# Seven running totals of a Strassen-style MLP product: which of them are quarters of the result, in which order the others are folded into them, and on which engine

## The chip, the cores and the metric

One core of a Trainium2 chip. The metric is the device time in microseconds of one execution, the median of the runs shown. Engines are called by the names of the profile: PE is TensorE, DVE is VectorE, ACT is ScalarE, POOL is GpSimd, SP is SyncE, whose queue starts all the transfers here.

## What is computed

One decoder layer on 1024 tokens of 1024 features in float32: an attention branch and an RWKV-7 branch, merged, then an MLP, then a gated per-layer embedding. The end of it, where the change lies:

```python
f = rmsnorm(h, ffn_pre_norm[i])
f = jnp.square(jax.nn.relu(f @ w_ff_in[i])) @ w_ff_out[i]     # 1024 -> 4096 -> 1024
h = h + rmsnorm(f, ffn_post_norm[i])
e = (p[i] @ w_ple[i]) * jax.nn.sigmoid(h @ w_ple_gate[i])
h = h + rmsnorm(e, ple_post_norm[i])
```

## The kernel before

**Precision.** Each float32 matmul is three matmuls of rounded operands (`mm3`, L250): high x high, high x low, low x high, into one PSUM bank of 128 x 512. An operand is split by ScalarE (a copy that rounds, the high part) and by VectorE or GpSimd (a subtraction, the low part).

**The MLP's second product.** The 4096 hidden features are taken in 16 chunks of 256 (`NP` = 16, p = 0 to 15). For a chunk the 1024 x 256 activations and the 256 x 1024 weights are cut into two by two quarters, and for the first 15 chunks Strassen's seven products replace the eight: each product of the order `MUL` (L1292) takes sums of quarters (`LEFT`, `RIGHT`; `prep` and `split2` make and split them ahead of time on GpSimd, ScalarE and VectorE) and gives four tiles of 128 x 512. `product` (L1371) multiplies them in five rotating PSUM banks and adds each to a running total of its own, `tot[1]` to `tot[7]`, on VectorE: the line `tot<-tot,bk` of the profile, called an eviction here. The last chunk, p = 15, is multiplied plainly, 16 tiles of six matmuls (`ff2_last`, L1435, three banks), added into the quarters of the result. `acc(i, c)` (L1308) says which total holds the quarter of token tile i and column half c.

**The folds.** With totals M1 to M7, the quarters are M1 + M4 - M5 + M7, M3 + M5, M2 + M4 and M1 - M2 + M3 + M6. In `product` of chunk 14 (the branch at L1385), after the products 4, 1 and 7, the totals are folded into the four that `acc` names: eight steps on four tiles of 128 x 512 each, 32 operations, the rows `tot<-tot,tot`; even tiles on GpSimd, odd ones on VectorE.

**Around them.** `ff1` (L1392) interleaves, for each 128 hidden features j, the first product (w_ff_in, banks `z`, two token halves of 24 matmuls) with the products of the chunk before: twelve matmuls of `z`, one product, and so on. So the last stretch of TensorE is: product 2, z, product 4, z, product 1, z, product 7, z, then the 16 tiles of `ff2_last`. `last_split` (L1325) splits the operands of chunk 15 beside them (`lhl` in four pieces on VectorE; `lwl` in two of 128 x 1024, the first on VectorE, the second on GpSimd). `last_weights` (L1450) loads w_ple_gate in eight pieces of 128 rows into two raw buffers (`wr`) and splits each: the left column half on GpSimd, the right half on VectorE (`wsplit`, L1177; rows `wpg<-wr,wpg`). `finish(i)` (L1476) normalises token tile i, adds the residual, and transposes it; `gate_mm(i)` (L1491) multiplies it by the gate weights, the left half first (24 matmuls), then the right half; `e_mm(i)` makes the output.

**Order.** TensorE's order is written out by the kernel's own planner (`Order`, with assumed durations). The context is entered with a manual schedule for TensorE alone:

```python
ctx.enter_context(tc.manual_schedule(engines={mybir.EngineType.PE}))   # L217
```

The queues of the other engines and of SP are ordered by the compiler. Each engine executes its queue in order. A buffer's `tag` says which storage it shares with earlier tiles: `last_split`'s second `lwl` takes the storage (`MP`) of the right operand of product 1, the gate weights' right halves take that of the second token half of f, which the last matmuls `z` read.

Of the kernel before, what the change touches and what calls it, by code (L numbers as in the profile page):

```python
# [13 lines left out]
OP = mybir.AluOpType  # L14
# [192 lines left out]
def layer(ctx: ExitStack, tc: tile.TileContext, x, pT, wz, wup, w_out, wff1, w_ff2, w_ple, w_pleg,  # L207
# [5 lines left out]
    V = Engine(nc.vector, sch, 0.18, 0.00104)  # L213
    S = Engine(nc.scalar, sch, 0.16, 0.00092)
    G = Engine(nc.gpsimd, sch, 0.15, 0.0022)
# [34 lines left out]
    def mm3(ps, pairs):  # L250
        n = len(pairs)
        for i, (ah, al, bh, bl) in enumerate(pairs):
            PE.matmul(ps, ah, bh, start=i == 0, stop=False)  # L253
            yield MM
            PE.matmul(ps, ah, bl, start=False, stop=False)  # L255
            yield MM
            PE.matmul(ps, al, bh, start=False, stop=i == n - 1)  # L257
            yield MM
# [142 lines left out]
    def rtile(shape, name, tag, dt=F32):  # L401
        n = 1
        for d in shape[1:]:
            n *= d
        assert n <= TAGN[tag], (shape, tag)
        return rt.tile(shape, dt, name=name, tag=tag, bufs=BUFS.get(tag, 1))
# [52 lines left out]
    for h in range(2):  # L459
        for n, t in ((0, xw), (1, xg)):  # L460
            ps = zl[h][n]
            c = slice(P_MUX + n, P_MUX + n + 1)
# [636 lines left out]
    def mtile(p, h, shape, name, dt):  # L1099
        return mgpool().tile(shape, dt, name=name, tag=f"mt{p}{h}")  # L1100
# [5 lines left out]
    def bank(tags=("s1", "s2", "s3")):  # L1106
        zi[0] += 1
        return psum.tile([128, 512], F32, name="bk", tag=tags[zi[0] % len(tags)])
# [156 lines left out]
    def mixed(i, ps):  # L1265
# [16 lines left out]
        for c in range(2):  # L1282
# [8 lines left out]
    NP = FF // 256  # L1291
# [2 lines left out]
            7: (2, 3, OP.subtract)}  # L1294
    RIGHT = {1: (0, 3, OP.add), 2: (0,), 3: (1, 3, OP.subtract), 4: (2, 0, OP.subtract), 5: (3,),
             6: (0, 1, OP.add), 7: (2, 3, OP.add)}
    tot = {}
    raw_h, raw_w, duo = {}, {}, {}
    last = {}

    def totals():
        for p, (x, y) in enumerate(((4, 3), (2, 6))):
            t = mtile("hl"[p], 1, [128, 2, 4, 512], f"tot{p}", F32)
            tot[x], tot[y] = t[:, 0], t[:, 1]
        for x, tag in ((1, "BT"), (5, "AR0"), (7, "AR1")):
            tot[x] = rtile([128, 4, 512], "tot", tag)

    def acc(i, c):  # L1308
        return tot[((4, 3), (2, 6))[i // 4][c]][:, i % 4]

    def ff1_half(ps, hi, lo, h):
        return mm3(ps, [(hi[:, k * 128:(k + 1) * 128], lo[:, k * 128:(k + 1) * 128],
# [2 lines left out]
    def ff1_evac(ps, j, h):  # L1315
        p, x = j // 2, 2 * (j % 2) + h
        if p not in raw_h:
            raw_h[p] = rtile([128, 4, 512], "hr", ("BK", "UV")[p % 2])
        f1 = rtile([128, 512], "f1", "gst")
        S.activation(f1, ps, AF.Relu)  # L1320
        S.activation(raw_h[p][:, x], f1, AF.Square)
        if x == 3 and p == NP - 1:
            last_split(1, (1,), ())

    def last_split(k, hs, ws):  # L1325

        if k not in last:
            if k == 0:
                last["h"] = rtile([128, 4, 512], "lh", "BK", F32R)
                last["w"] = rtile([128, 2, 1024], "lw", "BK2", F32R)  # L1330
            last[k] = (rtile([128, 2, 512], "lhl", ("Ep", "En")[k], F32R),
                       rtile([128, 1024], "lwl", ("kk", "MP")[k], F32R))
        for h in hs:
            x = 2 * k + h
            S.activation(last["h"][:, x], raw_h[NP - 1][:, x], AF.Copy)
            V.tensor_tensor(last[k][0][:, h], raw_h[NP - 1][:, x], last["h"][:, x], OP.subtract)
        for _ in ws:
            S.activation(last["w"][:, k], raw_w[NP - 1][k], AF.Copy)
            (G if k else V).tensor_tensor(last[k][1], raw_w[NP - 1][k], last["w"][:, k], OP.subtract)

    def load_w2(p):
        if p % 2:
# [18 lines left out]
    def prep(n):  # L1361
        p, i = n // 7, MUL[n % 7]
        if p >= NP - 1:
            return
        hq = [raw_h[p][:, x] for x in range(4)]
        wq = [raw_w[p][x // 2][:, halves[x % 2]] for x in range(4)]
        pick = lambda q, spec: [q[x] for x in spec[:2]] + list(spec[2:])
        duo[n] = (split2(pick(hq, LEFT[i]), ("Ep", "En", "a")[n % 3], ("ex", "py")[n % 2], V),
                  split2(pick(wq, RIGHT[i]), ("kk", "MP", "px")[n % 3], "pg", G))

    def product(n):  # L1371
        p, i = n // 7, MUL[n % 7]
        prep(n + 2)
        a, b = duo.pop(n)
        if not tot:
            totals()
        for t in range(4):
            ts = slice(t * 128, t * 128 + 128)
            ps = bank(("s1", "s2", "s3", "m0", "m1"))
            yield from mm3(ps, [(a[:, 0, ts], a[:, 1, ts], b[:, 0], b[:, 1])])  # L1380
            if p == 0:
                V.tensor_copy(tot[i][:, t], ps)
            else:
                V.tensor_tensor(tot[i][:, t], tot[i][:, t], ps, OP.add)
        if p == NP - 2:  # L1385
            for x, y, op in {4: ((6, 3, OP.add), (6, 2, OP.subtract), (3, 5, OP.add), (2, 4, OP.add),
                                 (4, 5, OP.subtract)),
                             1: ((6, 1, OP.add), (4, 1, OP.add)), 7: ((4, 7, OP.add),)}.get(i, ()):
                for t in range(4):
                    (V if t % 2 else G).tensor_tensor(tot[x][:, t], tot[x][:, t], tot[y][:, t], op)  # L1390

    def ff1(j):  # L1392
        def body(hi, lo):
# [41 lines left out]
    def ff2_last(i, c):  # L1435
        def body():
            h, ts = tok(i)
            ps = bank()
            yield from mm3(ps, [(last["h"][:, 2 * k + h, ts], last[k][0][:, h, ts], last["w"][:, k, halves[c]],
                                 last[k][1][:, halves[c]]) for k in range(2)])  # L1440
            V.tensor_tensor(acc(i, c), acc(i, c), ps, OP.add)
            if i + c == 0:
                last_weights()
            if c == 1:
                sch.spawn(finish(i), 1)
        sch.add(body)
# [29 lines left out]
    def finish(i):  # L1476
        yield from wait(lambda: i == 0 or i - 1 in hT and (i < 2 or ("G", i - 2) in done))
        a = [acc(i, 0), acc(i, 1)]
        r = ss2(a, [rtile([128, 512], "j", "gst") for c in range(2)])
        for c in range(2):  # L1480
            hl = rtile([128, 512], "hl", ("ex", "py")[c])
            SY.dma_start(hl, h_scr[i][:, halves[c]])
            V.scalar_tensor_tensor(a[c], a[c], r, P["g3"][:, halves[c]], op0=OP.mult, op1=OP.mult)
            V.tensor_tensor(a[c], a[c], hl, OP.add)
        yield sch.until(sch.dep + 0.3)
        hi = wpool.tile([128, KT, 128], F32R, name="wh")
        lo = wpool.tile([128, KT, 128], F32R, name="wl")
        yield from put_T(a, hi, lo, 0)
        hT[i] = (hi, lo, sch.dep + 0.1)
# [18 lines left out]
    def e_mm(i):  # L1508
        def body():
            ts = slice(i * 128, i * 128 + 128)  # L1510
            sg, eg = P["sg"][i % 4], P["eg"][i % 3]
            cols = halves if i < 7 else (halves[0], slice(512, 768), slice(768, 1024))
            sc = small.tile([128, 4], F32, name="sc")
            for n, c in enumerate(cols):
                ps = bank()[:, 0:c.stop - c.start]
                yield from mm3(ps, [(P["p"][0][k][:, ts], P["p"][1][k][:, ts], P["w"][0][k][:, c],
                                     P["w"][1][k][:, c]) for k in range(2)])
                V.tensor_tensor(sg[:, c], sg[:, c], ps, OP.mult)
                S.activation(ps, sg[:, c], AF.Square, accum_out=sc[:, n:n + 1])
                (V if n else G).tensor_tensor(eg[:, c], sg[:, c], P["g4"][:, c], OP.mult)  # L1520
                if n:
                    V.tensor_tensor(sc[:, n:n + 1], sc[:, n - 1:n], sc[:, n:n + 1], OP.add)
            r = rstd_of(sc[:, n:n + 1], "rs")
            for c in cols:
                V.scalar_tensor_tensor(sg[:, c], eg[:, c], r,
                                       acc(i, c.start // 512)[:, c.start % 512:(c.stop - 1) % 512 + 1], op0=OP.mult, op1=OP.add)
                SY.dma_start(out[i * 128:(i + 1) * 128, c], sg[:, c])
        sch.add(body, None, lambda: ("G", i) in done)
# [125 lines left out]
```

## Time and profile before

| | |
|---|---|
| median of 3 runs | 1854.36 us (1851.88 to 1858.59) |
| the profiled execution | 1856.02 us, its span 1854.2 us |
| TensorE busy | 1771.5 us (96%), 9392 matmuls |
| VectorE busy | 1072.1 us (58%) |
| ScalarE busy | 750.0 us (40%) |
| GpSimd busy | 717.0 us (39%) |
| mean granted TensorE clock | 0.978 of full speed |

Busy shares are means over the span. Times in the rows are microseconds from the start of the span; an arrow in brackets at the end of a row gives how long the engine was idle ahead of it and what released it.

### The profile page before, as it was taken

The numbers are of one execution on the slowest core, as the hardware profiler recorded it, in microseconds if no ns is written. First come the engines' busy times: TensorE is split into PE (matmuls) and PEld (weight loads), VectorE is DVE, ScalarE is ACT, GpSimd is POOL, SyncE is SP. The second block draws the span as 40 slices with busy tenths as digits, with TensorE's granted clock in tenths as the row PEclk, the third lists the DMA queues.
The fourth block names the chain that finished last, engine by engine and source line by source line (L and its number), as shares of the span: only waits on it lengthen the run. The fifth ranks groups of instructions, "written<-read, shape, count | busy, mean of one in ns | idle before, by whom it ended". The sixth has DMA issues, their size and how long they took to land.

```text
span 1854.2 us, 24541 instructions
## 1 busy us (share of the span) xinstructions
PE 1771.5 (96%) x9392; PEld 1425.7 (77%) x9392; DVE 1072.1 (58%) x2005; ACT 750.0 (40%) x1358; POOL 717.0 (39%) x475
## 2 busy tenths in 40 slices
PE   9998998899899999999999999999999999996998
PEld 8777777686677777777778788888888888885787
DVE  6375794967744333334753655555555555579654
ACT  5923334323344444344433533333333333333454
POOL 1422222121113233332230166666666666685301
PEclk9998999999999999999999999999999999998999
DMA  4621221121223222233542311111111111111321
GB/s 158 235 72 46 66 83 36 63 75 54 92 89 96 80 58 57 69 100 105 190 159 80 114 57 46 57 46 57 69 46 46 46 57 46 57 40 62 114 75 51
DMA packets 54999, 146.03 MB, mean 79 GB/s; under 512 B 6625, under 2 KB 13281, under 8 KB 54882
## 3 DMA queue, kind: packets, MB, share of 16 engines
q1 hardware_dynamic: 54882, 144.46, 23.4%
q8 instruction: 74, 1.21, 0.3%
q14 instruction: 43, 0.35, 0.1%
HBM read 110.49 MB, written 27.26 MB: 74 GB/s over the span
## 4 chain that ended last, share of the span: by engine, by line
PE 72%; DVE 8%; ACT 2%; issue 1%; POOL 1%; DMA 0%; DVEq 0%; SPq 0%; ACTq 0%; POOLq 0%
PE z L255 15%; PE z L257 15%; PE z L253 15%; PE bk L253 6%; PE bk L255 6%; PE bk L257 6%; DVE tot L100 1%; DVE xy L100 1%; PE po L236 1%; PE sc L236 1%; PE y L236 1%; DVE pt L100 1%; PE pt L244 1%; PE q L236 1%; PE tp L244 1%
## 5 line engine op out<-in xcount | busy, mean ns | idle before, releaser
L100 DVE TENSOR_TENSOR tot<-tot,bk 128x512 f32<-128x512 f32 x408 | 276.8, 686 | 225.9 <-PE bk L257 225.9
L100 POOL TENSOR_TENSOR wl<-wr,wh 128x1024 fp32r<-128x1024 f32 (+1 forms) x88 | 209.6, 2382 | 505.1 <-ACT wh L100 500.4
L253 PE MATMUL z<-uh,wh 128*128 128x512 f32 (+1 forms) x800 | 318.5, 398 | 2.6 <-ACT v L100 1.9
L255 PE MATMUL z<-ul,wh 128*128 128x512 f32 (+1 forms) x800 | 319.2, 399 | 0.3 <-DVE ul L100 0.3
L257 PE MATMUL z<-uh,wl 128*128 128x512 f32 (+1 forms) x800 | 319.2, 399 | 0.2 <-POOL wl L100 0.2
L253 PE MATMUL z<-f,wh 128*128 128x512 f32 x512 | 200.3, 391 | 1.9 <-ACT f L100 1.9
L255 PE MATMUL z<-f,wh 128*128 128x512 f32 x512 | 200.3, 391 | 0.2 <-DVE f L100 0.2
L257 PE MATMUL z<-f,wl 128*128 128x512 f32 x512 | 199.9, 390 | 0.0
L253 PEld LDWEIGHTS z<-uh,wh 128*128 128x128 f32 x800 | 152.8, 191 | 31.5 <-issue 3.4
L257 PEld LDWEIGHTS z<-uh,wl 128*128 128x128 f32 x800 | 152.9, 191 | 31.2 <-issue 5.4
L100 ACT ACTIVATE duo<-sum 128x512 fp32r<-128x512 f32 x150 | 89.5, 624 | 214.8 <-PE bk L257 122.6
L255 PEld LDWEIGHTS z<-ul,wh 128*128 128x128 f32 x800 | 152.8, 191 | 30.4 <-issue 5.3
L253 PE MATMUL bk<-duo 128*128 128x512 f32 x420 | 164.3, 391 | 7.3 <-DVE tot L100 7.3
L100 ACT ACTIVATE wh<-wr 128x1024 fp32r<-128x1024 f32 (+1 forms) x88 | 91.6, 1041 | 186.8 <-PE z L255 168.9
L255 PE MATMUL bk<-duo 128*128 128x512 f32 x420 | 164.1, 391 | 0.0
L257 PE MATMUL bk<-duo 128*128 128x512 f32 x420 | 164.1, 391 | 0.0
L100 POOL TENSOR_TENSOR duo<-sum,duo 128x512 fp32r<-128x512 f32 x75 | 99.7, 1330 | 129.6 <-ACT duo L100 127.7
L253 PEld LDWEIGHTS z<-f,wh 128*128 128x128 f32 x512 | 96.6, 189 | 22.3 <-ACT f L100 2.1
L255 PEld LDWEIGHTS z<-f,wh 128*128 128x128 f32 x512 | 96.7, 189 | 20.6 <-DVE f L100 0.5
L257 PEld LDWEIGHTS z<-f,wl 128*128 128x128 f32 x512 | 96.7, 189 | 20.1
L100 POOL TENSOR_TENSOR sum<-w2r 128x512 f32<-128x512 f32 x75 | 98.6, 1315 | 7.2 <-DVE oc L100 2.6
L253 PEld LDWEIGHTS bk<-duo 128*128 128x128 f32 x420 | 79.2, 189 | 24.1 <-DVE tot L100 7.7
(296 smaller groups left out, 3243.9 us busy)
## 6 DMA issues: line engine op xcount, KB each, us to landing
wr<-in_wz_dram SPq DMA_DIRECT2D x48, 512.0 KB, 3.5
w2r<-in_w_ff_dram SPq DMA_DIRECT2D x32, 512.0 KB, 3.6
wr<-in_wff_dram SPq DMA_DIRECT2D x32, 512.0 KB, 3.5
xt<-in_x_dram SPq DMA_DIRECT2D x16, 512.0 KB, 4.3
gscr<-gst SPq DMA_DIRECT2D x32, 256.0 KB, 2.0
g<-gscr SPq DMA_DIRECT2D x16, 512.0 KB, 4.7
sw<-qk SPq DMA_DIRECT2D x48, 128.0 KB, 2.3
sascr<-lst SPq DMA_DIRECT2D x16, 256.0 KB, 3.0
```

The source lines that it names most:

```text
L100: return f(*a, **kw)
L236: PE.matmul(out_, a, b, start=start, stop=stop)
L244: PE.transpose(out_, a, ident if idn is None else idn)
L253: PE.matmul(ps, ah, bh, start=i == 0, stop=False)
L255: PE.matmul(ps, ah, bl, start=False, stop=False)
L257: PE.matmul(ps, al, bh, start=False, stop=i == n - 1)
```

## The change

`totals` and `acc` now name the totals 7, 5, 4 and 6 as the quarters (5 and 4 end as M3 + M5 and M2 + M4, 7 and 6 as the two others) in place of 4, 3, 2 and 6; 2 and 3 take the storage that 5 and 7 had. The folds are regrouped: after product 4, three steps tile by tile on GpSimd; after product 1, one step on VectorE, then four on GpSimd; none after product 7. These are again eight steps, 32 operations: 28 on GpSimd and 4 on VectorE. The second `lwl` split goes from GpSimd to VectorE.

```diff
+    QUARTER = ((7, 5), (4, 6))
...
-        for p, (x, y) in enumerate(((4, 3), (2, 6))):
+        for p, (x, y) in enumerate(QUARTER):
             t = mtile("hl"[p], 1, [128, 2, 4, 512], f"tot{p}", F32)
             tot[x], tot[y] = t[:, 0], t[:, 1]
-        for x, tag in ((1, "BT"), (5, "AR0"), (7, "AR1")):
+        for x, tag in ((1, "BT"), (2, "AR0"), (3, "AR1")):
             tot[x] = rtile([128, 4, 512], "tot", tag)
 
     def acc(i, c):
-        return tot[((4, 3), (2, 6))[i // 4][c]][:, i % 4]
+        return tot[QUARTER[i // 4][c]][:, i % 4]
+
+    def gather(*steps, eng=G):
+        for t in range(4):
+            for x, y, op in steps:
+                eng.tensor_tensor(tot[x][:, t], tot[x][:, t], tot[y][:, t], op)
...
-            (G if k else V).tensor_tensor(last[k][1], raw_w[NP - 1][k], last["w"][:, k], OP.subtract)
+            V.tensor_tensor(last[k][1], raw_w[NP - 1][k], last["w"][:, k], OP.subtract)
...
         if p == NP - 2:
-            for x, y, op in {4: ((6, 3, OP.add), (6, 2, OP.subtract), (3, 5, OP.add), (2, 4, OP.add),
-                                 (4, 5, OP.subtract)),
-                             1: ((6, 1, OP.add), (4, 1, OP.add)), 7: ((4, 7, OP.add),)}.get(i, ()):
-                for t in range(4):
-                    (V if t % 2 else G).tensor_tensor(tot[x][:, t], tot[x][:, t], tot[y][:, t], op)
+            if i == 4:
+                gather((7, 5, OP.subtract), (5, 3, OP.add), (7, 4, OP.add))
+            if i == 1:
+                gather((6, 3, OP.add), eng=V)
+                gather((7, 1, OP.add))
+                gather((4, 2, OP.add), (6, 2, OP.subtract), (6, 1, OP.add))
```

## Rows read from the trace of the kernel before

**Rows 1.** Windows by stage: stretch, length, busy time of each engine, clock, transfers.

```profile
core 0: us, PE busy (x) PEld busy (x) DVE busy (x) ACT busy (x) POOL busy (x), PEclk, DMA share, GB/s
1680.00:1694.70 14.70, 7.40 (x23) 5.71 (x22) 14.70 (x13) 0.00 (x0) 11.73 (x7) 0.65 0.00 0
1694.70:1727.00 32.30, 24.92 (x100) 18.87 (x100) 28.82 (x45) 15.39 (x37) 10.59 (x8) 0.95 0.40 131
...
1744.00:1854.00 110.00, 102.94 (x485) 85.79 (x483) 50.39 (x96) 51.21 (x103) 10.34 (x8) 0.98 0.15 55
```

**Rows 2.** Timeline of TensorE: start, duration, what, count, idle time before and its releaser.

```profile
1676.70 0.39 PE L253 MATMUL z<-f,wh 128*128 128x512 f32 x1
...
1679.88 0.39 PE L257 MATMUL bk<-duo 128*128 128x512 f32 x1
1687.57 0.80 PE L253 MATMUL bk<-duo 128*128 128x512 f32 x1 [7.30 <-DVE tot L100]
...
1692.69 0.40 PE L253 MATMUL z<-f,wh 128*128 128x512 f32 x1
...
1726.77 1.03 PE L244 MATMUL tp<-cs,tot 128*128 128x128 f32 x8
1729.89 0.69 PE L253 MATMUL z<-wpg,wh 128*128 128x512 f32 x1 [2.09 <-ACT wh L100]
...
1733.63 0.40 PE L253 MATMUL z<-wpg,wh 128*128 128x512 f32 x1
...
1736.48 0.47 PE L253 MATMUL z<-wpg,wh 128*128 128x512 f32 x1
```

**Rows 3.** Timeline of VectorE from product 4's last eviction to product 7's.

```profile
1675.71 2.90 DVE L100 TENSOR_TENSOR tot<-tot,tot 128x512 f32<-128x512 f32 x2
...
1680.22 1.75 DVE L100 TENSOR_TENSOR tot<-tot,tot 128x512 f32<-128x512 f32 x1
1681.89 1.74 DVE L100 TENSOR_TENSOR lhl<-hr,lh 128x512 fp32r<-128x512 f32 x1
1683.56 3.35 DVE L100 TENSOR_TENSOR lwl<-w2r,lw 128x1024 fp32r<-128x1024 f32 x1
1686.84 2.47 DVE L100 TENSOR_TENSOR tot<-tot,bk 128x512 f32<-128x512 f32 x4
```

**Rows 4.** Timeline of GpSimd from 1647 to 1680 us.

```profile
1647.53 2.55 POOL L100 TENSOR_TENSOR sum<-hr 128x512 f32<-128x512 f32 x2
...
1653.87 3.04 POOL L100 TENSOR_TENSOR tot<-tot,tot 128x512 f32<-128x512 f32 x2 [0.35 <-DVE tot L100]
...
1660.28 3.00 POOL L100 TENSOR_TENSOR tot<-tot,tot 128x512 f32<-128x512 f32 x2
...
1673.34 6.41 POOL L100 TENSOR_TENSOR tot<-tot,tot 128x512 f32<-128x512 f32 x4
1679.71 3.37 POOL L100 TENSOR_TENSOR wpg<-wr,wpg 128x512 fp32r<-128x512 f32 x2
```

**Rows 5.** The totals' tile, 1500 us to the end: count, ns min/median/max, first and last start.

```profile
L100 DVE TENSOR_TENSOR tot<-tot,bk x144: 673/687/689, 1500.8 to 1728.2; 128x512 f32<-128x512 f32 x144
...
L100 POOL TENSOR_TENSOR tot<-tot,tot x14: 1272/1456/1750, 1653.9 to 1697.2; 128x512 f32<-128x512 f32 x14
```

**Rows 6.** The gate weights: timelines of VectorE, SP, ScalarE, GpSimd; last, DMA issues.

```profile
1699.59 0.68 DVE L100 TENSOR_TENSOR wpg<-wr,wpg 128x512 fp32r<-128x512 f32 x1
...
1707.73 1.37 DVE L100 TENSOR_TENSOR wpg<-wr,wpg 128x512 fp32r<-128x512 f32 x1 [1.13 <-ACT wpg L100]
...
1700.34 9.16 SPq L113 DMA_DIRECT2D wr<-in_w_pleg_dram  x4
...
1706.55 1.15 ACT L100 ACTIVATE wpg<-wr 128x512 fp32r<-128x512 f32 x2 [1.23 <-DMA wr<-in_w_pleg_dram]
...
1722.18 1.29 POOL L100 TENSOR_TENSOR wpg<-wr,wpg 128x512 fp32r<-128x512 f32 x1 [1.04 <-ACT wpg L100]
...
wr<-in_w_pleg_dram SPq DMA_DIRECT2D x7, 512.0 KB, 3.4
```

## The prediction

> **What bounds the kernel now.** I read the table of windows first, because the change lives in the last 200 us and an average over the span hides it. From 1744 us to the end TensorE is busy for 102.94 of 110 us [rows 1], so what happens earlier only moves that block; from 1680 to 1727 us it is not: 7.40 of 14.70 us and 24.92 of 32.30 us, with a mean granted clock of 0.65 in the first of the two. TensorE's own timeline says why [rows 2]. It stops at 1680.3 us for 7.30 us, released by VectorE's write of a total; a smaller one of 2.09 us stands ahead of the gate product of tile 0, which begins at 1729.89 us. After the first stop its clock is at the lower of its two levels: twelve matmuls take 5.12 us instead of 12 x 0.227 = 2.72 us (ahead of the stop, fourteen steps from 1676.70 to 1679.88 us, 0.227 us each). VectorE's timeline then shows what it did in that time [rows 3]: between the last eviction of product 4 and the first one of product 1 stand three folds (2.90 us for two, 1.75 us), two splits lhl (some 1.75 us each; the row shows one) and one split lwl (3.35 us), 11.1 us in all; the evictions for which TensorE waits begin only at 1686.84 us. GpSimd's timeline [rows 4] shows folds beside them, and shows that the order of the queues is not that of the code: two folds run at 1653.87 us, 14 us ahead of the product after which they are written. The compiler runs an instruction when its inputs are there, and of those that are ready I take it that the one written first goes first. Last, the tiles' view [rows 5, 6] has prices and the chain of the gate weights wpg.
>
> **VectorE's part.** 16 of the 32 folds are VectorE's now, four after the change (6 += 3, ready after product 6, so run where VectorE has time around 1656 us). In the stretch of the first stop the three folds leave, 2.90 + 1.75 = 4.65 us, and two folds that stand among the evictions ahead of it leave at least 2 x 0.69 = 1.4 us more, an estimate with VectorE's plain length [rows 5]. The first eviction of product 1 then comes at 1686.84 - 4.65 - 1.4 = 1680.8 us and takes 0.69 us, where TensorE stops at 1680.3: 1.2 us instead of 7.3, and without the low clock after it (5.12 - 2.72 = 2.4 us). The last matmul of w_ff_in is then done 8.5 us earlier, at 1686.2 instead of 1694.7 us (1692.69 + 9 x 0.227). The second lwl, moved to VectorE, costs it 1.3 us (twice 0.69) to 3.35 us [rows 3]; it reads a buffer that product 1's operands hold until its last matmul, so it falls between the evictions of products 1 and 7, where five banks cover it. If that cover is gone, it is a stop of at most 3.35 us. The last fold (4 += 7) vanishes from the end of the chain, since product 7 is now added into a quarter itself.
>
> **GpSimd's part.** Its 16 folds become 28, and it loses one lwl. Ready from about 1660.3 us on (product 5 is then evicted; a fold starts there now too [rows 4]), they come with three operand preparations that were there before: 31 operations of 512 columns. Alone one takes 1.28 us (2.55 us for two, with VectorE idle or on evictions); four folds beside four VectorE operations with both inputs in SBUF took 6.41 us, so 1.60 us each, and each VectorE operation cost GpSimd (6.41 - 4 x 1.275) / 4 = 0.33 us. Bounds: 31 x 1.28 = 39.5 us and 31 x 1.60 = 49.6 us. Between, I count VectorE's operations with two SBUF inputs in that time: two duo, four lhl, two wpg and two lwl counted double, 12 units x 0.33 = 4.0 us. I take 39.5 + 4.0 = 43.5 us, an estimate: the folds end at 1703.8 us. The waits that this adds: product 7's evictions now wait for 7 += 1 on GpSimd, its 19th operation, at 1660.3 + 19 x 1.40 = 1686.9 us. Queued behind them on VectorE are the last lhl, the second halves of the first wpg splits and the evictions of the last chunk. TensorE needs a bank of theirs for its second tile of the last chunk at 1686.2 + 6 x 0.227 = 1687.6 us: a wait of a microsecond or less.
>
> **The new bound is the gate weights.** The first two GpSimd splits wpg run at 1679.71 us now, in a hole between folds [rows 4]. They are written behind all folds, and after the change GpSimd always has a fold ready until 1703.8 us, so they come last. SP's load of the third 128 rows of w_ple_gate needs the first raw buffer, which that split and VectorE's split of the same rows release: now VectorE's is last, at 1699.59 us, and the load goes at 1700.34 us [rows 6]. After the change GpSimd's is last, 1703.8 + 1.3, and the load goes at 1705.1 us, nearly 5 us later than now. From there to the last GpSimd split it took 1723.47 - 1700.34 = 23.1 us; without VectorE's evictions between, a round is 3.4 (load) + 1.2 (two ScalarE halves) + 1.4 (splits, twice 0.69) = 6.0 us, and two rounds, one first half of 5.3 us (3.4 + 0.6 + 1.3) and one more split of 1.3 us make 18.6 us. I take the middle, 20.9 us: 1726.0 us. TensorE reaches that point long before: 1686.2 + 16 x 6 x 0.227 = 1708.0 us, so stops of some microseconds on its way cost nothing. After the last split stand three matmuls and the second half of gate product 0, 27 x 0.227 = 6.1 us, with a low clock that costs 1.7 us after the 2.09 us stop now (nine matmuls in 3.74 us [rows 2]) and so here too: 7.9 us, and the end of gate product 0 at 1733.9 us. Now it ends at 1736.48 + 30 x 0.227 = 1743.3 us, and everything behind it is TensorE's. **Sum: 1733.9 - 1743.3 = -9.4 us.** The profiled execution took 1856.0 us (span 1854.2), so 1846.6; it lies 1.7 us above the median of 1854.36, from which the forecast is **1845.0 us**. With the bounds together: folds at 1.28 us and 18.6 us give 1727.6, a gain of 15.7 (1838.7); folds at 1.60 us and 23.1 us give 1742.2, a gain of 1.1 (1853.3).
>
> **A rule to weigh.** Beside a fold of GpSimd, VectorE's operations with two SBUF inputs took 1.7 us instead of 0.69 (the lhl of [rows 3]), and GpSimd's folds up to 1.75 instead of 1.28 us [rows 5]. The Trainium skill, "SBUF — State Buffer", section "Who interferes with whom", speaks against this change: GpSimd and such a VectorE operation share a pair of ports as an exclusive lock, and the later one blocks until the first is done. By it GpSimd would lose a whole VectorE operation each time, and the sum would be that of rival 1. The trace agrees for VectorE, and for GpSimd it has half of that, 0.33 us.
>
> **Rivals.** (1) Each VectorE operation costs GpSimd its whole 0.69 us: 12 x 0.69 = 8.3 us, folds end at 1708.1, the load at 1709.4, gate product 0 at 1709.4 + 20.9 + 7.9 = 1738.2: a gain of 5.1, 1849.3 us, within the 0.3% (5.6 us) that a measurement of this kernel can tell from no change. For it: single folds at 1.75 us; against: the 0.33 us of four in a row. (2) The compiler does put the first wpg splits between the folds, as now. Then VectorE's half releases the load 5.6 us after the last matmul of w_ff_in (1700.34 - 1694.7), the weights are there by 1686.2 + 5.6 + 20.9 = 1712.7 us, and TensorE binds: 1708.0 + 1 for waits + 3.1 (from its transposes at 1726.77 to 1729.89 now) + 48 x 0.227 + 1.0 (eight more transposes) + 1.7 = 1725.7: a gain of 17.6, 1836.8 us. For it: they stand so today; against: today the folds are too few to fill GpSimd. (3) Slower: VectorE's queue is ordered with a wpg split of a late load ahead of evictions. Today one waits 1.13 us there [rows 6]. If the fifth of the eight splits stands ahead of eight or more of the sixteen last evictions, and folds take 1.60 us, the load at 1711.2 plus two rounds gives 1723.2; then eight tiles (8 x 1.36 = 10.9 us) and 3.1 + 13.6 us follow as in rival 2: 1750.8, 7.5 us slower, 1861.9 us. It makes the kernel slower from about three such evictions on, by over 0.3% from seven (each is worth 1.36 us). (4) That nothing comes of it: the 8.5 us are found but the chain of the weights eats all of them, which is the upper bound of the sum.
>
> **How the numbers follow.** The forecast with its bounds 0.55 (of it 0.08 within 0.3%), rival 1 0.15 (0.12 within), rival 2 0.15, rival 3 0.10 (0.07 slower by over 0.3%), rival 4 0.05 (0.02 of it slower). Faster 0.47 + 0.03 + 0.15 = 0.65, same 0.08 + 0.12 + 0.03 + 0.03 = 0.26, slower 0.09. The range 1838 to 1855 holds the forecast, rivals 1 and 4, and leaves out most of rival 2 and of rival 3.
>
> **What would show it.** Right: no stop of 7 us at product 7's second tile; GpSimd without a hole from 1660 to about 1704 us, with the first wpg splits at its end; the third wpg load at 1705 us; and a new stop of TensorE of 10 us or more ahead of or within gate product 0, put down to GpSimd's wpg. Wrong: wpg splits among the folds; folds at 1.28 us or at 1.75 us on the mean; VectorE waiting for GpSimd ahead of product 7's evictions for several microseconds; or a stretch after 1744 us that takes more than its 110 us.

## The result, and the profile after

| | before | after |
|---|---|---|
| median | 1854.32 us (1851.75 to 1859.05, 20 runs) | 1861.26 us (1857.75 to 1864.84, 20 runs) |
| the profiled execution (span) | 1856.02 us (1854.2) | 1858.71 us (1856.9) |
| TensorE busy in the span | 1771.5 us | 1770.9 us |

The ratio is 1.0037, with a 95% interval of 1.0029 to 1.0046: **slower by 6.9 us**, where 9.4 us faster was forecast, and above the range (1838 to 1855). The two profiled executions differ by only 2.7 us. At TensorE's 8600th matmul, in a `z` ahead of all folds, the profile of after stands at 1648.96 us and that of before at 1651.77, so 2.81 us of their difference have another source; they arise between 924 and 950 us, ahead of the MLP, where both do the same, so I take them for chance. From that matmul to the end it is 208.0 against 202.5 us. The expectations below count from it.

The windows of after, in the stretches of [rows 1] (columns as there):

```profile
1680.00:1694.70 14.70, 7.87 (x35) 6.20 (x33) 6.18 (x8) 2.67 (x5) 14.62 (x11) 0.92 0.00 0
1694.70:1727.00 32.30, 24.09 (x87) 18.62 (x88) 25.69 (x41) 12.83 (x32) 19.20 (x14) 0.82 0.40 125
1744.00:1857.00 113.00, 105.62 (x496) 88.03 (x494) 51.08 (x98) 51.62 (x103) 10.32 (x8) 0.98 0.16 56
```

In the first stretch VectorE and GpSimd have changed places: VectorE is busy for 6.18 us where it had no pause at all, GpSimd for 14.62 of 14.70 us. TensorE is busy for about as long as before (7.87 us for 7.40).

TensorE's timeline, the rows that answer to [rows 2], with each of its stops over 1.2 us from here to the end of gate product 0:

```profile
1674.41 0.50 PE L253 MATMUL bk<-duo 128*128 128x512 f32 x1 [2.40 <-DVE tot L100]
...
1686.12 0.39 PE L257 MATMUL z<-f,wl 128*128 128x512 f32 x1
...
1698.89 0.80 PE L253 MATMUL bk<-lw,lh 128*128 128x512 f32 x1 [11.02 <-DVE tot L100]
...
1706.42 0.50 PE L253 MATMUL bk<-lw,lh 128*128 128x512 f32 x1 [1.39 <-DVE tot L100]
...
1715.10 0.50 PE L253 MATMUL bk<-lw,lh 128*128 128x512 f32 x1 [2.49 <-DVE tot L100]
...
1727.72 1.03 PE L244 MATMUL tp<-cs,tot 128*128 128x128 f32 x8
...
1733.01 0.50 PE L257 MATMUL z<-wpg,wl 128*128 128x512 f32 x1 [2.37 <-DVE wl L100]
```

The stop of 7.30 us ahead of product 7's second tile is gone, and the last `z` matmul of w_ff_in stands at 1686.12 us. But a stop of 11.02 us has come two tiles into the last chunk (`bk<-lw,lh`). VectorE's timeline shows what it is (compare [rows 3]):

```profile
1672.95 0.81 DVE L100 TENSOR_TENSOR duo<-sum,duo 128x512 fp32r<-128x512 f32 x1 [8.60 <-ACT duo L100]
...
1680.58 2.47 DVE L100 TENSOR_TENSOR tot<-tot,bk 128x512 f32<-128x512 f32 x4
...
1683.66 2.31 DVE L100 TENSOR_TENSOR lwl<-w2r,lw 128x1024 fp32r<-128x1024 f32 x1
1694.48 0.69 DVE L100 TENSOR_TENSOR tot<-tot,bk 128x512 f32<-128x512 f32 x1 [8.52 <-POOL tot L100]
1696.92 0.69 DVE L100 TENSOR_TENSOR tot<-tot,bk 128x512 f32<-128x512 f32 x1 [1.75 <-POOL tot L100]
1698.15 0.69 DVE L100 TENSOR_TENSOR tot<-tot,bk 128x512 f32<-128x512 f32 x1 [0.54 <-POOL tot L100]
1700.61 0.69 DVE L100 TENSOR_TENSOR tot<-tot,bk 128x512 f32<-128x512 f32 x1 [1.77 <-POOL tot L100]
1701.21 1.15 DVE L100 TENSOR_TENSOR wpg<-wr,wpg 128x512 fp32r<-128x512 f32 x1
```

Product 1 is evicted at 1680.58 us without delay. Product 7's four evictions then wait for GpSimd, 8.52 us and three times more; TensorE goes on when the third is done, at 1698.84 us. Behind them in VectorE's queue stands the first right half of the gate weights. GpSimd's timeline (compare [rows 4]):

```profile
1658.74 1.29 POOL L100 TENSOR_TENSOR tot<-tot 128x512 f32<-128x512 f32 x1 [1.83 <-DVE tot L100]
...
1668.04 1.31 POOL L100 TENSOR_TENSOR sum<-w2r 128x512 f32<-128x512 f32 x1
...
1670.69 7.20 POOL L100 TENSOR_TENSOR tot<-tot,tot 128x512 f32<-128x512 f32 x5
1677.85 1.73 POOL L100 TENSOR_TENSOR duo<-sum,duo 128x512 fp32r<-128x512 f32 x1
1679.54 12.48 POOL L100 TENSOR_TENSOR tot<-tot,tot 128x512 f32<-128x512 f32 x8
1691.98 1.25 POOL L100 TENSOR_TENSOR wpg<-wr,wpg 128x512 fp32r<-128x512 f32 x1
1693.20 10.31 POOL L100 TENSOR_TENSOR tot<-tot,tot 128x512 f32<-128x512 f32 x8
1703.48 1.73 POOL L100 TENSOR_TENSOR wpg<-wr,wpg 128x512 fp32r<-128x512 f32 x1
...
1724.03 1.83 POOL L100 TENSOR_TENSOR wpg<-wr,wpg 128x512 fp32r<-128x512 f32 x1 [1.07 <-ACT wpg L100]
```

From 1658.74 us it works without a pause: 28 folds, three preparations of operands and a split in 44.7 us, 1.40 us each. The first eviction of product 7 starts 1.28 us after the last block of eight folds does, the others follow the blocks' steps: 7 += 1 stands in that last block, its first tile as GpSimd's 25th operation, its last as the 30th (the rows do not name the totals; this is read from the evictions' starts). Ahead of it are folds that are written behind it. ScalarE and SP add one row each: ScalarE waited for the operand sum that stands among the folds at 1668.04 us (this is where the stop of 2.40 us at product 1 comes from: ScalarE's duo, then VectorE's), and the third load of w_ple_gate starts behind VectorE's split of 1701.21 us (in [rows 6] at 1700.34):

```profile
1669.39 1.06 ACT L100 ACTIVATE lw<-w2r 128x1024 fp32r<-128x1024 f32 x1 [10.46 <-POOL sum L100]
```

```profile
1702.43 9.89 SPq L113 DMA_DIRECT2D wr<-in_w_pleg_dram  x4
```

### The profile page after: what moved, and what is told of

It reads as the page before. It is cut to its first block, busy times and chain, and to the rows that moved or that the text cites. A ratio compares the mean times of both kernels' runs of the same rounds, so it can differ in the third digit from the quotient of the medians.

```text
span 1856.9 us, 24544 instructions
## 1 busy us (share of the span) xinstructions
PE 1770.9 (95%) x9392; PEld 1425.7 (77%) x9392; DVE 1058.5 (57%) x1994; ACT 749.7 (40%) x1358; POOL 728.6 (39%) x486
## 3 DMA queue, kind: packets, MB, share of 16 engines
q8 instruction: 74, 1.21, 0.3%
## 4 chain that ended last, share of the span: by engine, by line
PE 70%; DVE 7%; POOL 3%; ACT 2%; issue 1%; DMA 1%; DVEq 0%; ACTq 0%; SPq 0%; POOLq 0%
PE z L255 15%; PE z L257 15%; PE z L253 15%; PE bk L253 6%; PE bk L257 6%; PE bk L255 6%; POOL tot L100 2%; DVE xy L100 1%; PE po L236 1%; PE sc L236 1%; PE y L236 1%; DVE pt L100 1%; DVE tot L100 1%; PE pt L244 1%; DMA g<-gscr 1%
## 5 line engine op out<-in xcount | busy, mean ns | idle before, releaser
L100 POOL TENSOR_TENSOR sum<-hr 128x512 f32<-128x512 f32 x75 | 96.3, 1293 | 2.3 <-ACT hr L100 2.3
```

Of the source, the lines that this page charges most:

```text
L100: return f(*a, **kw)
```

## The experiments

No kernel leaves work out. Theory A, the place: what costs is what stands behind the folds in the in-order queues of GpSimd and VectorE. Its rivals, the load: 28 folds on GpSimd cost what they cost in any order, since they slow VectorE beside them; or the new quarters, or the moved `lwl`, do it. Each ratio is against the kernel before, run beside it. The changed kernel itself stands at 1861.26 us and 1.0037 (1.0029 to 1.0046).

| run | edit | median, us | ratio (95%) |
|---|---|---|---|
| e1 | after; 7 += 1 on VectorE | 1857.53 | 1.0013 (1.0002 to 1.0024) |
| e2 | after; folds alternate between the engines | 1855.99 | 1.0005 (0.9995 to 1.0015) |
| e3 | before; all 32 folds on GpSimd | 1861.37 | 1.0030 (1.0017 to 1.0042) |
| e4 | after; 7 += 1 queued ahead of the last twelve folds | 1860.96 | 1.0035 (1.0021 to 1.0049) |
| e5 | after; the two last weight operands on VectorE | 1857.99 | 1.0019 (1.0009 to 1.0030) |
| e6 | e4 and e5 | 1857.89 | 1.0014 (1.0005 to 1.0024) |
| e7 | before; only the second lwl on VectorE | 1851.10 | 0.9983 (0.9973 to 0.9993) |
| e8 | after; last twelve folds queued behind the gate weights | 1861.54 | 1.0041 (1.0028 to 1.0054) |
| e10 | after; the second lwl back on GpSimd | 1866.06 | 1.0058 (1.0040 to 1.0076) |
| e11 | after; last twelve folds written behind the last eviction | 1853.09 | 0.9986 (0.9977 to 0.9995) |
| e12 | e11 and e5 | 1850.07 | 0.9974 (0.9965 to 0.9983) |
| e13 | e12, and those folds behind the gate weights too | 1852.74 | 0.9986 (0.9973 to 1.0000) |

**e1, one step back on VectorE.**

```diff
-                gather((7, 1, OP.add))
+                gather((7, 1, OP.add), eng=V)
```

> The changed kernel with one edit: the fold 7 += 1 (four operations) runs on VectorE, the other 24 stay on GpSimd. Theory A (the loss is the wait of product 7's evictions for 7 += 1, which GpSimd runs behind 24 other operations): the wait of 8.5 us on VectorE shrinks to under 5 us, since 7 += 1 now waits for 7 += 4 on GpSimd alone (at about 1681 to 1688 us), the stop of TensorE falls from 11 us to 3 to 6 us, and the time falls by 5 to 9 us to about 1853 us. Theory B (the loss is not that wait but the slower VectorE and GpSimd beside each other and late operand preparations on GpSimd): the wait only changes its name, and the time stays at 1859 to 1862 us.

Measured 1857.53 us, between the two forecasts: some two thirds of the loss are back (1.0037 to 1.0013). The stop of 11.02 us is gone, and another has come. TensorE's timeline, then VectorE's:

```profile
1696.55 0.79 PE L255 MATMUL bk<-lwl,lh 128*128 128x512 f32 x1 [7.45 <-DVE lwl L100]
```

```profile
1686.28 3.46 DVE L100 TENSOR_TENSOR tot<-tot,tot 128x512 f32<-128x512 f32 x2 [1.23 <-POOL tot L100]
...
1694.22 2.28 DVE L100 TENSOR_TENSOR lwl<-w2r,lw 128x1024 fp32r<-128x1024 f32 x1
```

The four folds now stand in VectorE's queue ahead of `lwl`, wait there for GpSimd's 7 += 4, and TensorE waits for `lwl`. The wait for GpSimd has moved to the next instruction in the queue.

**e2, the engines alternate as before**, with the new quarters, order and `lwl`.

```diff
-                eng.tensor_tensor(tot[x][:, t], tot[x][:, t], tot[y][:, t], op)
+                (V if t % 2 else G).tensor_tensor(tot[x][:, t], tot[x][:, t], tot[y][:, t], op)
```

> The changed kernel with the new quarters and the new grouping, but each step on both engines, odd tiles on VectorE and even ones on GpSimd, as before the change. Theory A (the placing on GpSimd makes the wait of 8.5 us): GpSimd has 16 folds again, 7 += 1 is done soon after product 1's evictions, no wait of VectorE for GpSimd over 2 us; the 7.3 us stop of before comes back in part, as VectorE has folds ahead of product 1's evictions again: 1851 to 1856 us. Theory C (the new quarters themselves cost, as product 7 now has to wait for other folds): 1858 us or more also here.

Measured 1855.99 us, no difference from before and 5 us below after: so what makes after slower than before is the engine of the folds. That the new quarters cost nothing does not follow, since this run has the moved `lwl` as well, which is a gain when it is alone (e7 below).

**e3, the old quarters and order, all on GpSimd.**

```diff
-                    (V if t % 2 else G).tensor_tensor(tot[x][:, t], tot[x][:, t], tot[y][:, t], op)
+                    G.tensor_tensor(tot[x][:, t], tot[x][:, t], tot[y][:, t], op)
```

> The kernel before with one edit: all 32 folds on GpSimd, with the old quarters 4, 3, 2 and 6 and the old order. Theory A: the evictions of product 7 wait for nothing here, as total 7 is no quarter, and the 7.3 us stop is gone; but the first eviction of the last chunk waits for 4 += 7 on GpSimd, behind 28 folds and two splits, until about 1703 us, and TensorE stops there with three banks full: the wait has moved behind product 7, and the time is 1858 to 1866 us. Theory C (new quarters cost, the placing does not): the stop at product 1 is gone and nothing takes its place: 1846 to 1850 us.

Measured 1861.37 us, as slow as after and in the range of theory A, by a wait of the same kind but not at the place that I had named (4 += 7): the second `lwl` stands on GpSimd behind folds, and TensorE stops for it.

```profile
1701.33 0.80 PE L255 MATMUL bk<-lwl,lh 128*128 128x512 f32 x1 [13.78 <-POOL lwl L100]
```

**e4, 7 += 1 ahead of the last twelve folds** on GpSimd; `issue_after` queues the block's instructions behind the one given.

```diff
...
-                gather((7, 1, OP.add))
-                gather((4, 2, OP.add), (6, 2, OP.subtract), (6, 1, OP.add))
+                with tc.issue_after(gather((7, 1, OP.add))):
+                    gather((4, 2, OP.add), (6, 2, OP.subtract), (6, 1, OP.add))
```

> The changed kernel with one edit in the order of GpSimd's queue: the steps 4 += 2, 6 -= 2 and 6 += 1 are queued behind 7 += 1, so that 7 += 1 is GpSimd's 16th to 21st operation there and not its 24th to 32nd. The number of folds on each engine is unchanged. Theory A (the loss is product 7's evictions waiting for a 7 += 1 that GpSimd runs too late): product 7's last eviction ends at about 1690 us instead of 1701, the stop of 11 us falls under 3 us, and the time falls by 7 to 11 us below the changed kernel's 1861.3, to 1850 to 1854 us. Theory B (28 folds on GpSimd cost by contention and late operands, wherever they stand): 1858 to 1862 us.

Measured 1860.96 us, no faster than after. The 11.02 us are gone as forecast (2.55 us are left of them), but the loss is not, and theory A's 1850 to 1854 us failed. GpSimd's, VectorE's and TensorE's timelines:

```profile
1692.05 21.42 POOL L100 TENSOR_TENSOR tot<-tot,tot 128x512 f32<-128x512 f32 x14
1713.43 2.50 POOL L100 TENSOR_TENSOR wpg<-wr,wpg 128x512 fp32r<-128x512 f32 x2
```

```profile
1705.57 3.43 DVE L100 SCALAR_TENSOR_TENSOR tot<-tot,rs,g 128x512 f32<-128x512 f32 x2
1708.93 3.41 DVE L100 TENSOR_TENSOR tot<-tot,hl 128x512 f32<-128x512 f32 x2
...
1719.30 1.34 DVE L100 TENSOR_TENSOR wpg<-wr,wpg 128x512 fp32r<-128x512 f32 x1 [5.77 <-ACT wpg L100]
```

```profile
1694.10 0.80 PE L253 MATMUL bk<-lw,lh 128*128 128x512 f32 x1 [2.55 <-DVE tot L100]
...
1712.99 0.79 PE L253 MATMUL bk<-lw,lh 128*128 128x512 f32 x1 [6.67 <-DVE tot L100]
1721.30 0.80 PE L253 MATMUL bk<-lw,lh 128*128 128x512 f32 x1 [3.21 <-DVE tot L100]
```

Now the twelve folds hold the gate weights up: GpSimd has no time for the splits after the second until 1713.43 us, the raw buffers stay taken, and VectorE stands 5.77 us at a split of a late load with evictions queued behind it. That is my third rival, in its own place; and beside the folds VectorE's steps of `finish` take 1.7 us each instead of 0.7. This run could not tell whether place or load does it.

**e5 and e6, the operands of products 1 and 7 on VectorE**, alone and with e4.

```diff
-            G.tensor_tensor(t, *src)
+            (G if eng is not V or spare != "pg" else V).tensor_tensor(t, *src)
...
-                  split2(pick(wq, RIGHT[i]), ("kk", "MP", "px")[n % 3], "pg", G))
+                  split2(pick(wq, RIGHT[i]), ("kk", "MP", "px")[n % 3], "pg", V if n > 7 * NP - 10 else G))
```

> The changed kernel with the weight operands of its last two products (a sum and a split for each of products 1 and 7 of chunk 14) prepared on VectorE instead of GpSimd: four operations that in the changed kernel stand behind folds. Theory B (the late operands are the loss): the 8.6 us for which VectorE waits for an operand and the 2.4 us stop of TensorE at product 1's operands vanish, and most of the 7 us loss with them: 1854 to 1856 us. Theory A (7 += 1 is the loss): 7 += 1 comes some 5 us earlier, as GpSimd has four operations less, and the 11 us stop falls to 5 to 8 us: 1856 to 1859 us, with the stop at the last chunk's second tile still the largest.

> The two edits together: 7 += 1 ahead of the folds that nobody waits for, and the last two weight operands on VectorE. Theory A: what the forecast assumed now holds, that is no stop of 7 us at product 7 and no wait of VectorE for GpSimd over 2 us; VectorE's queue of the last chunk then starts some 12 us earlier than in the changed kernel, and the time is 1846 to 1851 us, below the kernel before. Theory D (the last chunk is bound by the gate weights behind VectorE's own splits and not by product 7's evictions): 1853 us or more.

Measured 1857.99 and 1857.89 us. In e5, moving four operations out from between the folds is worth about half of the loss: the stop of 2.40 us at product 1 goes. The time is theory A's, but the long stop is still 9.83 us where it asked for 5 to 8. With e4 added, nothing more comes that can be told (the intervals overlap). The forecast of 1846 to 1851 us for e6 failed and theory D's number came: as in e4, fourteen folds stand ahead of the late gate splits, VectorE waits 5.80 us at one of these, and TensorE stops for 6.66 and 3.31 us.

**e7, the smallest part of the change alone**, on the kernel before.

```diff
-            (G if k else V).tensor_tensor(last[k][1], raw_w[NP - 1][k], last["w"][:, k], OP.subtract)
+            V.tensor_tensor(last[k][1], raw_w[NP - 1][k], last["w"][:, k], OP.subtract)
```

> The kernel before with the smallest part of the change alone: the second split lwl on VectorE instead of GpSimd. All theories: it lies between the evictions of products 1 and 7, covered by five banks; 1853 to 1857 us, no difference from before. If it costs 1.3 to 3.4 us, the cover is missing.

Measured 1851.10 us: this part is a gain, against both kernels, where I had expected no difference. With GpSimd idle beside it VectorE's split takes 1.21 us. The first `lwl`, which took 3.35 us in the kernel before [rows 3], beside GpSimd's `lwl` (2.78 us from 1683.05 us on), takes 1.21 us here too, and the stop of 7.30 us at the products is 5.15. VectorE's timeline, then TensorE's:

```profile
1691.65 1.21 DVE L100 TENSOR_TENSOR lwl<-w2r,lw 128x1024 fp32r<-128x1024 f32 x1
```

```profile
1684.04 0.80 PE L253 MATMUL bk<-duo 128*128 128x512 f32 x1 [5.15 <-DVE tot L100]
```

**e8 and e10.** In e8 the folds of tokens 512 to 1023 (totals 4 and 6, not finished until long after) are taken out of `product` and put into `last_weights`, behind its loop, where `last_g` is GpSimd's split of the last piece; e10 undoes e7's part in the changed kernel.

```diff
...
+        with tc.issue_after(last_g):
+            gather((4, 2, OP.add), (6, 2, OP.subtract), (6, 1, OP.add))
         P["g3"] = rtile([128, D], "g3", "v")
```

> The changed kernel with its last twelve folds (4 += 2, 6 -= 2, 6 += 1, all of tokens 512 to 1023) written behind the splits of the gate weights and queued on GpSimd behind the last of them; nothing is left out and GpSimd keeps its 28 folds. Theory A (what costs is what stands behind the folds in the two queues: product 7's evictions behind 7 += 1, the gate weights' splits behind the rest): 7 += 1 ends near 1688 us, the stop of 11 us at product 7 falls under 2 us, the third load of the gate weights goes before 1698 us, gate product 0 ends 87 to 91 us after matmul 8600 (96.9 in the changed kernel, 87.1 with the lwl move alone), and the run takes 1846 to 1852 us, ratio 0.996 to 0.999. Theory B (28 folds on GpSimd cost what they cost wherever they stand, since they slow VectorE's operations beside them): the loss moves behind 1727 us, where the tiles are finished, and the run takes 1856 to 1861 us.

> The changed kernel with the second split lwl put back on GpSimd; nothing is left out. If the folds' place in GpSimd's queue is the cause, lwl comes behind folds there as in the kernel before with all folds on GpSimd (1861.4 us): TensorE stops over 10 us for it at the first tile of the last chunk, and the run takes 1861 to 1866 us. If moving lwl to VectorE was itself what hurt (it stands ahead of product 7's evictions there), the run takes 1854 to 1858 us.

e8 took 1861.54 us: my forecast for it failed, and the time is that of the rival (1856 to 1861 us). Yet the gate weights were as early as theory A had it: GpSimd's last split ends at 1714.35 us, where the folds begin (its timeline first, then VectorE's and TensorE's).

```profile
1714.35 18.86 POOL L100 TENSOR_TENSOR tot<-tot,tot 128x512 f32<-128x512 f32 x12
```

```profile
1716.52 1.74 DVE L100 TENSOR_TENSOR wpg<-wr,wpg 128x512 fp32r<-128x512 f32 x1
1718.19 0.67 DVE L100 TENSOR_TENSOR tot<-tot,bk 128x512 f32<-128x512 f32 x1
1720.67 1.28 DVE L100 TENSOR_TENSOR tot<-tot,bk 128x512 f32<-128x512 f32 x2 [1.81 <-POOL tot L100]
```

```profile
1718.92 0.80 PE L253 MATMUL bk<-lw,lh 128*128 128x512 f32 x1 [8.68 <-DVE tot L100]
```

The folds are still written ahead of the evictions of tiles 4 to 7, which add into the same totals; so these must wait for them, now at 1714 us and later. e10 took 1866.06 us, with a stop of 17.44 us put down to GpSimd's `lwl`: this part of the change should not be undone (its interval and that of after just overlap).

**e11, the same folds with no eviction behind them.** An eviction and a fold both add to the total, so their order is free (up to rounding); taken out of `product` as in e8, the folds are written in `ff2_last` behind the last eviction. e12 adds the edit of e5.

```diff
...
+            if i + c == 8:
+                gather((4, 2, OP.add), (6, 2, OP.subtract), (6, 1, OP.add))
             if c == 1:
```

> As the run with the last twelve folds queued behind the gate weights, but the folds are also written behind the last eviction of the last chunk, so that no eviction has to wait for a fold of its total; nothing is left out and GpSimd keeps its 28 folds. Theory A (in that run the sixteen evictions of the last chunk and the steps of finish stood in VectorE's queue behind totals that GpSimd still had to fold, 8.7 us for the longest stop of TensorE; the place is what costs): no stop over 3 us in the last chunk, the last weights split by 1714 us, gate product 0 ends 78 to 87 us after matmul 8600, and the run takes 1843 to 1850 us, ratio 0.994 to 0.998. Theory B (28 folds on GpSimd cost what they cost wherever they stand, by slowing VectorE's steps of finish beside them from 0.7 to 1.7 us): the loss moves once more, behind the last eviction, and the run takes 1855 to 1861 us.

> The same, and in addition the sum and the split of the last two weight operands of the products (of products 1 and 7) go to VectorE, as in the earlier run with the late operands there. Theory A: the stop of 2.4 us at product 1's first tile, for which VectorE waits since GpSimd's operand sum stands among folds, is gone too, and the run is 1 to 4 us faster than the one before it, 1841 to 1848 us. Theory B: 1854 to 1860 us; if VectorE has no room for four more operations there, the stop comes back as one for VectorE and the run is no faster than the one before it.

e11 took 1853.09 us: **the same 28 folds on GpSimd and 4 on VectorE, in another place, and 8 us of difference** (1.0037 and 0.9986), from slower than before to a little faster. The theory that the load costs the same in any place falls with it. It is no more than e7 has with one line moved (0.9983): in this place the folds on GpSimd cost nothing that can be told, and gain nothing. GpSimd's and SP's timelines show the next splits soon after the upper half's folds, the lower half's from 1711.9 us on, and the third load at 1695.20 us instead of 1702.43 (10 us earlier, counted from the 8600th matmul):

```profile
1691.32 2.49 POOL L100 TENSOR_TENSOR tot<-tot,tot 128x512 f32<-128x512 f32 x2
1699.55 1.29 POOL L100 TENSOR_TENSOR wpg<-wr,wpg 128x512 fp32r<-128x512 f32 x1 [5.74 <-ACT wpg L100]
...
1714.25 4.38 POOL L100 TENSOR_TENSOR tot<-tot,tot 128x512 f32<-128x512 f32 x3 [1.04 <-DVE ss L100]
1718.60 1.74 POOL L100 TENSOR_TENSOR wpg<-wr,wpg 128x512 fp32r<-128x512 f32 x1
```

```profile
1695.20 9.01 SPq L113 DMA_DIRECT2D wr<-in_w_pleg_dram  x4
```

But the forecast of 1843 to 1850 us was too good by 3 us: a stop of 4.29 us stayed in the last chunk where I had allowed 3, and the last split was done at 1723.70 us and not by 1714, since some folds stood ahead of it. e12 came 3.0 us under e11, as forecast, though 2 us above its own range. It is the fastest kernel measured, ahead of before and after; e7's interval, with one line moved, overlaps it.

**e13, e12 with those folds also behind the gate weights.** In e11 and e12 some folds slip in ahead of the last splits; here they cannot.

```diff
...
-                gather((4, 2, OP.add), (6, 2, OP.subtract), (6, 1, OP.add))
+                with tc.issue_after(P["last_g"]):
+                    gather((4, 2, OP.add), (6, 2, OP.subtract), (6, 1, OP.add))
```

> The run with the lower half's folds behind the last eviction and the late operands on VectorE, with those twelve folds also queued on GpSimd behind its last split of a gate weight; nothing is left out. There, GpSimd had put four folds ahead of the last two splits (5.6 us) and one between them, and VectorE's steps of finish ran at 1.2 to 1.8 us beside them, with TensorE stopping 3.1 and 2.0 us at gate product 0. Theory A (place in the queue): the last split comes 5 us earlier, the steps of finish ahead of gate product 0 are plain again, gate product 0 ends 2 to 5 us earlier (84.2 us after matmul 8600 there), and the run takes 1845 to 1849 us. Rival: GpSimd's last split was not what TensorE waited for (the transposes of tile 0 are behind the sixteenth tile in its own order), the folds only move behind and slow the finish of tile 1 instead: 1849 to 1852 us, no difference that can be told.

Measured 1852.74 us, not faster than e12 (the intervals overlap). The last split ended where the folds begin (GpSimd's timeline), 3.5 us earlier than in e12, counted from the 8600th matmul, and TensorE stopped in the last chunk as long as in e11:

```profile
1713.77 16.44 POOL L100 TENSOR_TENSOR tot<-tot,tot 128x512 f32<-128x512 f32 x10
```

```profile
1704.11 0.50 PE L253 MATMUL bk<-lw,lh 128*128 128x512 f32 x1 [4.37 <-DVE tot L100]
```

So theory A fails for this last piece: the splits no longer set the end, and the rival came closest (1849 to 1852 us). Its mechanism shows in part: in the two profiles e13 is 4.0 us longer than e12 from the 8600th matmul on, and 2.2 us of that come after gate product 0, where the folds now stand. What bounds e12 is open. VectorE is busy for 24.66 of the 28.52 us of its last chunk, and for 30.41 of the 32.30 us from 1694.70 us on, a stretch from the middle of the last chunk into gate product 0. That points to VectorE, but it is argued from the rows and was not tried.

```profile
1686.28:1714.80 28.52, 24.38 (x97) 18.80 (x96) 24.66 (x40) 15.49 (x37) 16.81 (x13) 0.94 0.43 131
1694.70:1727.00 32.30, 24.41 (x92) 18.79 (x91) 30.41 (x41) 13.79 (x30) 25.67 (x17) 0.84 0.49 158
```

## Why the prediction was wrong

Times of this section are in the clock of before's profile, so 2.8 us later than in the rows of after.

**Right, or nearly.** The stop of 7.30 us went. The last `z` matmul ended at 1689.2 us (1694.7 before, 1686.2 forecast): 5.5 us of the 8.5, since a stop of 2.40 us stands at product 1 in place of the 1.2 us forecast, with some 1.7 us for the lower clock behind it, which the forecast had put at nothing; the stop is GpSimd's late operand. GpSimd's pace was 1.40 us for each operation, as forecast; it began 1.2 us later, had one gate split more to do, and its folds end at 1706.3 us (1703.8 forecast). The third load of the gate weights went at 1705.2 us (1705.1), if by VectorE's half and not GpSimd's, and the last split was done at 1728.7 us (1726.0).

**The step that failed first** is that 7 += 1 is GpSimd's "19th operation", and so "a wait of a microsecond or less" for product 7's evictions. It rested on my reading that of the ready instructions "the one written first goes first". The trace has 7 += 1 as the 25th to 30th operation, behind folds that are written after it, and TensorE stops for 11.02 us. The pace was right and the place wrong. e4 shows it: with 7 += 1 ahead of the rest 2.55 us of the stop are left, though the loss moves on. The same reading gave "so they come last" for the first two gate splits; one stood among the folds.

**The step that failed second** made it dear: "TensorE reaches that point long before", at 1708.0 us, "so stops of some microseconds on its way cost nothing". For the last chunk TensorE needed 41.4 us (1686.35 to 1727.72 in the rows) instead of 21.8: its stops are 11.02 + 1.39 + 2.49 = 14.9 us, and most of the other 4.7 us is the lower clock (behind the first and the last of them some eight matmuls each are 0.43 us apart instead of 0.227). The 21.8 us were 96 matmuls without a stop, and the trace of before already spoke against them: there the last chunk took 32.0 us (1694.74 to 1726.77), with a stop of 4.89 us that the prediction does not list:

```profile
1713.35 0.79 PE L253 MATMUL bk<-lw,lh 128*128 128x512 f32 x1 [4.89 <-DVE tot L100]
```

No run came near them: the shortest last chunk is that of e12, 28.5 us. In after, TensorE arrived at 1730.5 us, 1.9 us after the last split: the slack of 18 us between 1708.0 and 1726.0 was used up, and all 48 matmuls of gate product 0 came after it, not the last 27. Gate product 0 ended at 1748.9 us, not 1733.9. These 15.0 us are the miss of the forecast (16.3 us between the medians); behind gate product 0 both profiles take 111.1 us. The stop of 10 us or more at gate product 0, by which the new bound was to show, is not there: the stops are 1.16 and 2.37 us, and neither is put down to GpSimd's `wpg`.

**The unknown cost of the lock** was not the question: with folds at 1.28 us each GpSimd's 28th operation, for which the third eviction of product 7 waits, would still end at 1661.5 + 28 x 1.28 = 1697.4 us (an estimate), some 7 us after TensorE came to a stop at 1690.5. Rival 1 is only a size. Rival 3 named the right place, VectorE's queue, and by chance the right time (1861.9 us), but its mechanism, a late split ahead of evictions, ran in e4, not in the changed kernel. What I had asked for as a sign that I was wrong, VectorE waiting several microseconds for GpSimd ahead of product 7's evictions, is what the trace shows.

**Where the expected gain is.** The change has two parts that pull against each other: `lwl` on VectorE gains (e7; e10 points the other way), the folds on GpSimd lose (from 0.9983 in e7 to 1.0037), unless they stand where e11 puts them (0.9986). No run shows a gain from the folds on GpSimd themselves. The choice of quarters was not run alone. e2 has the new quarters and steps with the moved `lwl`, and stands above e7 (1.0005 against 0.9983, the intervals apart): together they cost some 4 us there. But the new quarters make possible what e11 uses: after 7 += 4 no fold reads totals 4 and 6, so their own folds can wait until after the last chunk. The kernel before can do so only with 6 += 1: its 6 -= 2 must come before 2 += 4, and that before 4 -= 5.

## What to carry to other kernels

- Work moved to an idle engine lands in an in-order queue. List what waits for each moved operation, and ask of the compiled queue, not of the source, how many operations stand ahead of it; if it matters, state the order.
- Removing the wait that a trace shows moved the loss three times here (e1, e4, e8). What paid was to take the dependency away (e8 to e11, 8 us): additions into one total can be made in any order, up to rounding, so the late ones go where nobody waits.
- A slack on one chain is spent by the stops of the other. Add the stops up before calling them free, those that the trace of before already has among them.
- Run the smallest part of a change alone. One line moved (e7) was worth as much here as the best placing of all the folds (e11).

## What the hardware showed that I had not expected

- Two float32 operations of 128 x 512 with both inputs in SBUF, one on VectorE and one on GpSimd, went in step. In e4 four steps of `finish` stand beside folds and nothing else: 3.43 + 3.41 us for the four, and three folds beside them in 5.04 us (GpSimd's timeline), so 1.7 us for each on either engine. Alone two such steps took 1.28 us (after, at 1713.17 us) and two folds 2.49 us (e11). So VectorE lost 1.0 us for each and GpSimd 0.4, somewhat more than the 0.33 us of the prediction. The Trainium skill, "SBUF — State Buffer", section "Who interferes with whom", calls the ports that the two engines share an exclusive lock. The trace is near that: a pair takes 1.7 us, where one after the other would take 0.64 + 1.25 = 1.9 us.

```profile
1706.75 5.04 POOL L100 TENSOR_TENSOR tot<-tot,tot 128x512 f32<-128x512 f32 x3
```

- A larger operation waits too: the split of 128 x 1024 took 1.21 us on VectorE with GpSimd idle (e7) and 2.31 us beside folds (after, at 1683.66 us).
- Two profiles of kernels with the same work up to 1650 us stood 2.81 us apart there, nearly as much as parts of this change are worth (e7: 3.2 us). The profiles place a stop; the ratios of many runs weigh it.
